# A streaming log-sum-exp prefix: straight-line engines, and a last store split between two queues

## The chip, the cores and the metric

The kernel runs on one core of a Trainium2 chip. The metric is device microseconds of one execution, as the device measures it. Each kernel was run several times, and medians are quoted. The profile is of one of these executions, and its span (first to last instruction) is some 1.7 us shorter than the time of the same execution.

## The reference

A running log-sum-exp along the second axis of a float32 tensor of 8 x 4096 x 2048. It is 268.44 MB in and as much out.

```python
out[:, 0, :] = x[:, 0, :].copy()
for t in range(1, S):
    mx = np.maximum(out[:, t - 1, :], x[:, t, :])
    out[:, t, :] = mx + np.log(np.exp(out[:, t - 1, :] - mx) + np.exp(x[:, t, :] - mx))
```

## The kernel before

The input is cut into 64 tiles of 512 rows: 128 partitions, 4 rows each, 2048 columns, 4 MB in and 4 MB out ("8 MB per tile" below counts both). Six buffers rotate. SyncE (SP) loads. ScalarE (ACT) takes the exponential, VectorE adds the four rows of a partition, TensorE adds what lies in the partitions above and carries the sum into the next tile. VectorE joins the two, ScalarE takes the logarithm and issues the store. SP, ACT and DVE run in loops, so that each wait subtracts its count from the semaphore:

```python
def take(engine, s, n):
    event(engine, [(s, n)], [(s, "sem-sub-imm", n)])
...
with nc.Block() as block:
    ...
    @block.sync
    def _(sp):
        ...
        sp.dma_start(out=ti[0][:, 0:2, :], in_=x_v[0][:, 0:2, :]).then_inc(top, 16)
        sp.dma_start(out=ti[0][:, 2:R, :], in_=x_v[0][:, 2:R, :]).then_inc(loaded[0], 16)
        ...
        with sp.Fori(1, turns + 1) as j:
            for n in range(NI):
                take(sp, stored[n], 16)
                load(x_v[bass.ds(j * NI + n, 1)][0], n)
```

The last two tiles leave as column halves. Such a half has 4 KB rows in HBM:

```python
def store(n, dst, turn, h=None):
    cols = slice(0, D) if h is None else half(h)
    act.wait_ge(logs, 2 * turn + (2 if h is None else h + 1))
    act.dma_start(
        out=dst[:, :, cols], in_=ti[n % NI][:, :, cols]
    ).then_inc(stored[n % NI], 16)
...
for h in range(2):
    ln(NT - 1, h, NT - 1 - first)
    store(NT - 1, o_v[NT - 1], NT - 1 - first, h)
```

The softmax here doesn't subtract the row's maximum and nothing guards it: scores larger than these inputs give would overflow.

## Time and profile before

| | before |
|---|---|
| median of the first 3 runs | 1250.83 us (1250.73 to 1252.3) |
| span of the profiled execution | 1249.03 us |
| end of the last data packet in it | 1247.33 us |
| from there to the end of the span ("exit") | 1.70 us |
| DMA rate from 10 to 1208 us | 433 GB/s, all 16 engines busy |

How to read it: the DMA engines are full from 2 us on (first packet at 2.04 us, share 1.00 from 2 to 10 us), so only three things can move the time. They are the start of the first load, the rate of the middle, and the last few microseconds, in which the DMA engines finish one after another. The prediction below shows the lines.

The trace does not number the DMA engines. What it has are packets with start, length, size and queue, and a four-byte completion packet per engine at the end of each transfer (1040 for 65 loads, 16 each). While the engines are full (share 1.00 from 10 to 1208 us), an engine's next packet starts as the one before it ends, so packets can be strung together.

### The profile page before, as it was taken

To read this page: it belongs to the slowest core of one execution; us is meant where nothing else is said; L and a number is where in the kernel's file an instruction comes from. 1 tells how busy PE (TensorE), PEld (TensorE's weight loads), DVE (VectorE), ACT (ScalarE), POOL (GpSimd) and SP (SyncE) were. 2 spreads that over 40 slices of the span, in tenths; PEclk is the share of its full clock that TensorE was granted. 3 is DMA by queue.
4 is the path that set the end of the run, shared out by engine and by line. 5 is a ranking of instruction groups with operands and counts; after the bars stand their busy time and mean duration, and the time that the engine had idled before them with its cause. 6 is when DMAs were issued, how large, how long until landed. Compare 5 with 4: busy or idle time off the path is not lost. (4 is left out here: it accounts for less than half of the span.)

```text
span 1249.0 us, 3456 instructions
## 1 busy us (share of the span) xinstructions
PE 650.8 (52%) x960; PEld 215.3 (17%) x960; DVE 1023.0 (82%) x512; ACT 907.2 (73%) x258; POOL 1.1 (0%) x8
## 2 busy tenths in 40 slices
PE   3556455554566545655455544565545564465541
PEld 1112111111112111211111111121111121111110
DVE  4999978778787787887878878778787787877873
ACT  5897866867768677686776866867768677686774
POOL 0000000000000000000000000000000000000000
PEclk9897778786887868778778786777878878678785
DMA  9999999999999999999999999999999999999998
GB/s 403 420 436 430 433 430 437 433 431 434 430 436 434 431 433 430 437 434 430 434 430 436 436 430 434 430 436 437 428 434 431 436 436 429 434 430 436 436 430 354
DMA packets 20409, 537.01 MB, mean 430 GB/s; under 512 B 2096, under 2 KB 2096, under 8 KB 4144
## 3 DMA queue, kind: packets, MB, share of 16 engines
q1 hardware_dynamic: 9360, 268.44, 49.9%
q10 hardware_dynamic: 11040, 268.44, 49.9%
q8 instruction: 7, 0.11, 0.0%
q14 instruction: 2, 0.02, 0.0%
HBM read 268.44 MB, written 268.44 MB: 430 GB/s over the span
## 5 line engine op out<-in xcount | busy, mean ns | idle before, releaser
L136 ACT ACTIVATE ti<-ti 128x4096 f32<-128x4096 f32 (+1 forms) x128 | 452.6, 3582 | 310.2 <-ACTq L59 304.2
L232 DVE TENSOR_TENSOR ti<-ti 128x1024 f32<-128x1024 f32 x384 | 464.7, 1224 | 200.0 <-ACT ti L136 191.3
L241 DVE TENSOR_TENSOR ti<-ti,ps 128x4096 f32<-128x4096 f32 x128 | 560.0, 4416 | 9.4 <-PE ps L208 9.0
L208 PE MATMUL ps<-ti,before 128*128 128x512 f32 x512 | 380.4, 895 | 342.6 <-DVE ti L232 342.1
L142 ACT ACTIVATE ti<-ti 128x4096 f32<-128x4096 f32 x128 | 455.4, 3602 | 11.5 <-PE ps L197 6.0
L197 PE MATMUL ps<-ti,last 128*128 128x512 f32 x448 | 270.6, 735 | 234.2 <-DVE ti L241 234.2
L208 PEld LDWEIGHTS ps<-ti,before 128*128 128x128 f32 x512 | 128.7, 279 | 609.0 <-DVE ti L232 500.9
L197 PEld LDWEIGHTS ps<-ti,last 128*128 128x128 f32 x448 | 86.6, 214 | 401.8 <-DVE ti L241 334.7
L159 ACT ACTIVATE ti<-ti 128x4096 f32<-128x4096 f32 x1 | 3.6, 3616 | 6.5 <-ACTq L59 6.5
L32 ACT ACT_TABLE_LOAD x1 | 1.3, 1283 | 0.8 <-PEq L274 0.8
L103 POOL TENSOR_SCALAR_AFFINE_SELECT last<-last 128x128 f32<-128x128 f32 x1 | 0.3, 296 | 0.0
L98 POOL TENSOR_SCALAR_AFFINE_SELECT before<-before 128x128 f32<-128x128 f32 x1 | 0.3, 295 | 0.1
L95 POOL MEMSET last<- 128x128 f32 x1 | 0.2, 206 | 0.0
L94 POOL MEMSET before<- 128x128 f32 x1 | 0.2, 205 | 0.5 <-SPq L77 0.5
L274 POOL MEMSET const-bfloat16-1.0<- 128x1 bf16 x1 | 0.1, 103 | 0.0
L274 POOL MEMSET const-uint8-127<- 128x1 uint8 x1 | 0.1, 103 | 0.0
L274 POOL MEMSET const-float32-0.0<- 128x1 f32 x1 | 0.1, 99 | 0.3 <-issue 0.3
L274 POOL MEMSET const-float32-1.0<- 128x1 f32 x1 | 0.1, 99 | 0.0
## 6 DMA issues: line engine op xcount, KB each, us to landing
ti<-in_x_dram SPq DMA_DIRECT2D x63, 4096.0 KB, 38.4
out_dram<-ti ACTq DMA_DIRECT2D x62, 4096.0 KB, 44.0
out_dram<-ti ACTq DMA_DIRECT2D x4, 2048.0 KB, 12.9
ti<-in_x_dram SPq DMA_DIRECT2D x2, 2048.0 KB, 9.7
```

The lines of the kernel that those rows point to most:

```text
L32: nc.scalar.preload_act_table_set("natural_log_exp_and_others")
L94: g.memset(before[:], 1.0).then_inc(ones, 1)
L98: g.affine_select(out=before[:], in_=before[:], compare_op=mybir.AluOpType.is_ge, fill=0.0, base=-1, pattern=[[1, P]], channel_multiplier= ...
L103: g.affine_select(out=last[:], in_=last[:], compare_op=mybir.AluOpType.is_ge, fill=0.0, base=-(P - 1), pattern=[[0, P]], channel_multiplier=1,
L136: act.activation(t[:, rows, half(h)], t[:, rows, half(h)], ACT.Exp).then_inc(exps[h], 1)
L142: act.activation(t[:, :, half(h)], t[:, :, half(h)], ACT.Ln)._wait_ge(carried[h], turn + 1).then_inc(logs, 1)
L159: act.activation(ti[0][:, 0:2, :], ti[0][:, 0:2, :], ACT.Exp)
L197: m = pe.matmul(ps[(n + 1) % 2][:, sl], last[:], ti[n % NI][:, R - 1, sl], start=True, stop=False, skip_group_check=True,)
L208: m = pe.matmul(ps[n % 2][:, sl], before[:], ti[n % NI][:, R - 1, sl], start=n % NBLK == 0, stop=True, skip_group_check=True,)
L232: a = dve.tensor_add(t[:, r, half(h)], t[:, r - 1, half(h)], t[:, r, half(h)])
L241: dve.tensor_add(t[:, :, half(h)], t[:, :, half(h)], ps[n % 2][:, half(h)].unsqueeze(1).to_broadcast([P, R, HALF]),)._wait_ge(ahead[h], n ...
L274: nc = _bacc.Bacc("TRN2", target_bir_lowering=False, num_devices=1)
```

## The change

Its intent has three parts. The loops of SP, ACT and DVE are unrolled and the subtracting waits become plain ones. Tile 62 leaves whole, and tile 63 by rows (row 0, row 1, rows 2 and 3). And the last of these, 2 MB, is split by partitions: 60 of them leave through GpSimd's queue, which is meant to use 15 of the 16 DMA engines and leave out the slow one. A copy of five partitions at the head is meant to place the gap.

```diff
+    def parts(n):
+        return [slice(0, 1), slice(1, 2), slice(2, R)] if n == NT - 1 else [slice(0, R)]
+    PASS = slice(64, 124)
...
+        for rows, c in ((slice(0, 2), top), (slice(2, R), loaded[0])):
+            c(nc.sync.dma_start(out=ti[0][:, rows, :], in_=x_v[0][:, rows, :]), 16)
         with nc.Block() as block:
...
+                aimed(g.dma_start(out=spare[0:5, 64:80], in_=spare[0:5, 0:16]), 16)
+                g.wait_ge(aimed.s, aimed.n)
+                g.wait_ge(final.s, 1)
+                rows = parts(NT - 1)[-1]
+                passed(g.dma_start(
+                    out=o_v[NT - 1][PASS, rows, :], in_=ti[(NT - 1) % NI][PASS, rows, :]
+                ), 16)
...
             def _(sp):
-                with sp.Fori(1, turns + 1) as j:
-                    for n in range(NI):
-                        take(sp, stored[n], 16)
-                        load(x_v[bass.ds(j * NI + n, 1)][0], n)
+                for n in range(1, NT):
+                    i = n % NI
+                    if n >= NI:
+                        sp.wait_ge(stored[i].s, n // NI * 16)
+                    loaded[i](sp.dma_start(out=ti[i][:], in_=x_v[n]), 16)
...
             def _(act):
+                                for own in (
+                                    [slice(0, PASS.start), slice(PASS.stop, P)] if end else [slice(0, P)]
+                                ):
+                                    stored[n % NI](act.dma_start(
+                                        out=o_v[n][own, rows, :], in_=t[own, rows, :]
+                                    ), 16)
...
+        for c in [*stored, passed]:
+            nc.sync.wait_ge(c.s, c.n)
```

(Cut to its core. The same is done to DVE's and ACT's loops and to all waits.)

More of the change, by code (lines that the diff above doesn't have):

```diff
@@ L36 @@
     R = 4
+    NI = 6
+    FD = 512
+    HALF = D // 2
     NBLK = S // (P * R)
     NT = B * NBLK
-    FD = 512
-    NI = 6
-    HALF = D // 2
-    assert NI % 2 == 0 and NBLK % 2 == 0 and D == 4 * FD
+    assert D == 4 * FD
     pool = ctx.enter_context(tc.tile_pool(name="io", bufs=1))
@@ L47 @@
     last = pool.tile([P, P], f32, name="last", tag="last")
+    spare = pool.tile([P, P], f32, name="spare", tag="spare")
     ti = [pool.tile([P, R, D], f32, name=f"ti{i}", tag=f"ti{i}") for i in range(NI)]
@@ L52 @@
     o_v = out.rearrange("b (k p r) d -> (b k) p r d", p=P, r=R)
-    def half(h):
-        return slice(h * HALF, (h + 1) * HALF)
-    def event(engine, waits, updates):
-        engine.add_instruction(mybir.InstEventSemaphore(
-            name=f"I-{nc.next_id()}", engine=engine.engine, ins=[], outs=[],
-            sync_info=mybir.SyncInfo(
-                on_wait=[mybir.SyncWait(
-                    sync_type="semaphore", id=s.num, ant_name=s.name,
-                    wait_mode="sem-ge-imm", wait_value=n,
-                ) for s, n in waits],
-                on_update=[mybir.SyncUpdate(
-                    sync_type="semaphore", id=s.num, ant_name=s.name,
-                    update_mode=mode, update_value=n,
-                ) for s, mode, n in updates],
-            ),
-        ))
@@ L73, in take, with __init__, __call__ @@
-    def take(engine, s, n):
-        event(engine, [(s, n)], [(s, "sem-sub-imm", n)])
+    half = [slice(h * HALF, (h + 1) * HALF) for h in range(2)]
+    def parts(n):
+        return [slice(0, 1), slice(1, 2), slice(2, R)] if n == NT - 1 else [slice(0, R)]
+    PASS = slice(64, 124)
+    class Count:
+        def __init__(self, name):
+            self.s, self.n = tc.alloc_semaphore(name), 0
+        def __call__(self, inst, by=1):
+            inst.then_inc(self.s, by)
+            self.n += by
+            return self.n
@@ L77, with counts @@
     with tc.tile_critical():
-        def sems(name, n):
-            return [nc.alloc_semaphore(f"{name}{i}") for i in range(n)]
-        ones, shaped, logs, top = (
-            sems(s, 1)[0] for s in ("ones", "shaped", "logs", "top")
-        )
-        loaded, stored = sems("loaded", NI), sems("stored", NI)
-        exps, chain, sums, ahead, joined, carried = (
-            sems(s, 2) for s in ("exps", "chain", "sums", "ahead", "joined", "carried")
-        )
+        def counts(name, n):
+            return [Count(f"{name}{i}") for i in range(n)]
@@ new lines @@
+        ones, shaped, logs, top, chain, aimed, final, passed = (
+            Count(s) for s in ("ones", "shaped", "logs", "top", "chain", "aimed", "final", "passed")
+        )
+        loaded, stored = counts("loaded", NI), counts("stored", NI)
+        exps, sums, ahead, joined, carried = (
+            counts(s, 2) for s in ("exps", "sums", "ahead", "joined", "carried")
+        )
+        for rows, c in ((slice(0, 2), top), (slice(2, R), loaded[0])):
+            c(nc.sync.dma_start(out=ti[0][:, rows, :], in_=x_v[0][:, rows, :]), 16)
@@ L93, in _ @@
             def _(g):
-                g.memset(before[:], 1.0).then_inc(ones, 1)
-                g.memset(last[:], 1.0).then_inc(ones, 1)
-                g.wait_ge(ones, 2)
-                g.affine_select(
+                ones(g.memset(before[:], 1.0))
+                ones(g.memset(last[:], 1.0))
+                ones(g.memset(spare[:], 0.0))
+                g.wait_ge(ones.s, ones.n)
+                shaped(g.affine_select(
                     out=before[:], in_=before[:], compare_op=mybir.AluOpType.is_ge, fill=0.0,
@@ L100, in _ @@
                     base=-1, pattern=[[1, P]], channel_multiplier=-1,
-                ).then_inc(shaped, 1)
-                g.affine_select(
+                ))
+                shaped(g.affine_select(
                     out=last[:], in_=last[:], compare_op=mybir.AluOpType.is_ge, fill=0.0,
                     base=-(P - 1), pattern=[[0, P]], channel_multiplier=1,
-                ).then_inc(shaped, 1)
+                ))
+                aimed(g.dma_start(out=spare[0:5, 64:80], in_=spare[0:5, 0:16]), 16)
@@ L108, in _ @@
+                g.wait_ge(aimed.s, aimed.n)
[4 more added lines that the diff above has]
+                ), 16)
             @block.sync
             def _(sp):
-                def load(src, n):
-                    sp.dma_start(out=ti[n][:], in_=src).then_inc(loaded[n], 16)
-                sp.dma_start(out=ti[0][:, 0:2, :], in_=x_v[0][:, 0:2, :]).then_inc(top, 16)
@@ L115, in _ @@
-                sp.dma_start(out=ti[0][:, 2:R, :], in_=x_v[0][:, 2:R, :]).then_inc(loaded[0], 16)
-                for n in range(1, NI):
-                    load(x_v[n], n)
-                turns = (NT - NI) // NI
-                with sp.Fori(1, turns + 1) as j:
-                    for n in range(NI):
-                        take(sp, stored[n], 16)
-                        load(x_v[bass.ds(j * NI + n, 1)][0], n)
-                for n in range((turns + 1) * NI, NT):
-                    take(sp, stored[n % NI], 16)
-                    load(x_v[n], n % NI)
@@ L126, in _, with exp @@
-                for n in range(NT - NI, NT):
-                    take(sp, stored[n % NI], 32 if n >= NT - 2 else 16)
+                for n in range(1, NT):
[3 more added lines that the diff above has]
+                    loaded[i](sp.dma_start(out=ti[i][:], in_=x_v[n]), 16)
             @block.scalar
             def _(act):
-                def exp(n, h, rows=slice(0, R)):
+                def exp(n):
                     t = ti[n % NI]
-                    if h == 0:
-                        take(act, loaded[n % NI], 16)
-                    act.activation(
-                        t[:, rows, half(h)], t[:, rows, half(h)], ACT.Exp
-                    ).then_inc(exps[h], 1)
@@ L140, in ln @@
-                def ln(n, h, turn):
-                    t = ti[n % NI]
-                    act.activation(
-                        t[:, :, half(h)], t[:, :, half(h)], ACT.Ln
-                    )._wait_ge(carried[h], turn + 1).then_inc(logs, 1)
-                def store(n, dst, turn, h=None):
-                    cols = slice(0, D) if h is None else half(h)
-                    act.wait_ge(logs, 2 * turn + (2 if h is None else h + 1))
-                    act.dma_start(
-                        out=dst[:, :, cols], in_=ti[n % NI][:, :, cols]
-                    ).then_inc(stored[n % NI], 16)
@@ L153, in settle @@
-                def settle(turns):
-                    take(act, carried[0], turns)
-                    take(act, carried[1], turns)
-                    take(act, logs, 2 * turns)
-                take(act, top, 16)
-                act.activation(ti[0][:, 0:2, :], ti[0][:, 0:2, :], ACT.Exp)
-                exp(0, 0, slice(2, R))
-                exp(0, 1, slice(2, R))
-                turns = (NT - 2) // NI
-                with act.Fori(0, turns) as j:
-                    for n in range(1, NI + 1):
-                        exp(n, 0)
-                        exp(n, 1)
-                        ln(n - 1, 0, n - 1)
-                        ln(n - 1, 1, n - 1)
-                        store(n - 1, o_v[bass.ds(j * NI + (n - 1), 1)][0], n - 1)
-                    settle(NI)
@@ L171, in _ @@
-                first = turns * NI
-                for n in range(first + 1, NT):
-                    up, turn = n - 1, n - 1 - first
-                    exp(n, 0)
-                    if n < NT - 1:
-                        exp(n, 1)
-                    ln(up, 0, turn)
-                    if n == NT - 1:
-                        store(up, o_v[up], turn, 0)
-                        exp(n, 1)
-                    ln(up, 1, turn)
-                    store(up, o_v[up], turn, 1 if n == NT - 1 else None)
@@ L183, in _ @@
-                for h in range(2):
-                    ln(NT - 1, h, NT - 1 - first)
-                    store(NT - 1, o_v[NT - 1], NT - 1 - first, h)
-                settle(NT - first)
+                    lo = 0
+                    if n == 0:
+                        lo = 2
+                        act.activation(t[:, :lo], t[:, :lo], ACT.Exp)._wait_ge(top.s, 16)
+                    for h in range(2):
+                        a = act.activation(t[:, lo:, half[h]], t[:, lo:, half[h]], ACT.Exp)
+                        if h == 0:
+                            a._wait_ge(loaded[n % NI].s, (n // NI + 1) * 16)
+                        exps[h](a)
@@ new lines, in ln @@
+                def ln(n):
+                    t = ti[n % NI]
+                    for h in range(2):
+                        for rows in parts(n) if h else [slice(0, R)]:
+                            end = n == NT - 1 and rows.stop == R and h == 1
+                            c = final if end else logs
+                            c(act.activation(
+                                t[:, rows, half[h]], t[:, rows, half[h]], ACT.Ln
+                            )._wait_ge(carried[h].s, n + 1))
+                            if h:
+                                act.wait_ge(c.s, c.n)
+                                for own in (
[4 more added lines that the diff above has]
+                                    ), 16)
@@ L188, in _ @@
+                exp(0)
+                for n in range(NT):
+                    if n + 1 < NT:
+                        exp(n + 1)
+                    ln(n)
             @block.tensor
@@ L192, in carry @@
                     if n % NBLK == NBLK - 1:
-                        event(pe, [(joined[h], n + 1)], [(carried[h], "sem-add-imm", 1)])
+                        pe.wait_ge(joined[h].s, n + 1)
+                        pe.sem_inc(carried[h].s, 1)
                         return
@@ L201, in carry @@
                         if c == 2 * h:
-                            m._wait_ge(joined[h], n + 1)
-                    m.then_inc(carried[h], 1)
+                            m._wait_ge(joined[h].s, n + 1)
+                    carried[h](m)
                 def triangle(n, h):
@@ L212, in triangle @@
                         if c == 2 * h:
-                            m._wait_ge(sums[h], n + 1)
-                    m.then_inc(ahead[h], 1)
-                pe.wait_ge(shaped, 2)
+                            m._wait_ge(sums[h].s, n + 1)
+                    ahead[h](m)
+                pe.wait_ge(shaped.s, shaped.n)
                 for n in range(NT):
@@ L222, in _ @@
                         carry(n, h)
-                for h in range(2):
-                    take(pe, sums[h], NT)
-                    take(pe, joined[h], NT)
             @block.vector
@@ L229, in local @@
                 def local(n, h):
-                    t = ti[n]
+                    t, cols = ti[n % NI], half[h]
                     for r in range(1, R):
-                        a = dve.tensor_add(t[:, r, half(h)], t[:, r - 1, half(h)], t[:, r, half(h)])
+                        a = dve.tensor_add(t[:, r, cols], t[:, r - 1, cols], t[:, r, cols])
                         if r == 1:
-                            a._wait_ge(exps[h], n + 1)
+                            a._wait_ge(exps[h].s, n + 1)
                         else:
-                            a._wait_ge(chain[h], (R - 2) * n + r - 1)
-                        a.then_inc(*((chain[h], 1) if r < R - 1 else (sums[h], 1)))
+                            a._wait_ge(chain.s, chain.n)
+                        (chain if r < R - 1 else sums[h])(a)
                 def join(n, h):
-                    t = ti[n]
-                    dve.tensor_add(
-                        t[:, :, half(h)], t[:, :, half(h)],
-                        ps[n % 2][:, half(h)].unsqueeze(1).to_broadcast([P, R, HALF]),
-                    )._wait_ge(ahead[h], n + 1).then_inc(joined[h], 1)
-                def turn(tiles):
-                    for n in range(tiles):
-                        for h in range(2):
-                            local(n, h)
-                        for h in range(2):
-                            join(n, h)
-                    for h in range(2):
-                        take(dve, exps[h], tiles)
-                        take(dve, chain[h], (R - 2) * tiles)
-                        take(dve, ahead[h], tiles)
-                with dve.Fori(0, NT // NI):
-                    turn(NI)
-                turn(NT % NI)
+                    t, cols = ti[n % NI], half[h]
+                    joined[h](dve.tensor_add(
+                        t[:, :, cols], t[:, :, cols],
+                        ps[n % 2][:, cols].unsqueeze(1).to_broadcast([P, R, HALF]),
+                    )._wait_ge(ahead[h].s, n + 1))
+                for n in range(NT):
+                    for h in range(2):
+                        local(n, h)
+                    for h in range(2):
+                        join(n, h)
+        for c in [*stored, passed]:
+            nc.sync.wait_ge(c.s, c.n)
 _INS = ['x']
```

## The prediction

> **What bounds the kernel now.** I read the page first: engine shares, then the row of DMA slices, then the queues.
>
> ```profile
> PE 650.8 (52%) x960; PEld 215.3 (17%) x960; DVE 1023.0 (82%) x512; ACT 907.2 (73%) x258; POOL 1.1 (0%) x8
> ...
> DMA  9999999999999999999999999999999999999998
> ...
> DMA packets 20409, 537.01 MB, mean 430 GB/s; under 512 B 2096, under 2 KB 2096, under 8 KB 4144
> ...
> q1 hardware_dynamic: 9360, 268.44, 49.9%
> q10 hardware_dynamic: 11040, 268.44, 49.9%
> q8 instruction: 7, 0.11, 0.0%
> ```
>
> No compute engine is full; the 16 DMA engines are, in every slice but the last. Loads (q1) and stores (q10) each take half of them. The work is 268.44 MB in and 268.44 MB out, so the time is a head before the first byte, 537 MB through full DMA engines, and a tail. Next the stretches, to see whether the stream ever thins:
>
> ```profile
> 0.00:10.00 10.00, 0.00 (x0) 0.00 (x0) 0.00 (x0) 2.66 (x2) 1.09 (x8) 1.00 0.80 315
> 10.00:1208.00 1198.00, 641.52 (x948) 212.27 (x948) 1005.82 (x504) 883.03 (x251) 0.00 (x0) 0.79 1.00 433
> 1208.00:1244.00 36.00, 9.25 (x12) 3.03 (x12) 17.13 (x9) 21.48 (x6) 0.00 (x0) 0.65 0.99 418
> 1244.00:1249.00 5.00, 0.00 (x0) 0.00 (x0) 0.00 (x0) 0.00 (x0) 0.00 (x0) 0.50 0.11 47
> ```
>
> The last two columns are DMA share and GB/s. From 10 to 1244 us the DMA is full (1.00 and 0.99). In the last 5 us it is at 0.11 while no engine computes. Magnified, the last 10 us in slices of 0.25 us:
>
> ```profile
> DMA  9999999989999999987655330000000000000000
> GB/s 426 393 442 410 426 410 442 442 360 442 393 459 410 393 442 410 442 360 311 246 213 229 131 131 16 33 16 33 33 16 33 16 33 0 0 0 0 0 0 0
> ```
>
> The rate steps down from 1243.5 to 1245 as engines finish one after another, then stays at 16 to 33 GB/s until 1247.25. A sixteenth of 430 GB/s is 27: **one DMA engine works alone for 2.2 us.** The trace's packets say the same. Each transfer ends with a four-byte completion packet per DMA engine; for the last store these come at 1243.35 us for the first, 1245.13 for the fifteenth and 1247.32 for the sixteenth. In the first load the sixteenth was only 0.17 us behind the fifteenth; over the last 35 tiles that distance grows by some 0.06 us per tile of 8 MB, except where another engine is delayed. So I read one engine as 0.3% slower than the rest (0.06 of 19.36 us per tile), always the last, and its share of the bytes sets the end. Last, the timeline:
>
> ```profile
> 1231.86 0.54 ACTq L149 DMA_DIRECT2D out_dram<-ti  x1
> 1232.54 3.62 ACT L142 ACTIVATE ti<-ti 128x4096 f32<-128x4096 f32 x1 [0.71 <-PEq L59]
> 1236.18 0.54 ACTq L149 DMA_DIRECT2D out_dram<-ti  x1
> ```
>
> The last logarithm ends at 1236.16, eleven microseconds before the last byte. The arithmetic at the end is hidden by a queue of stores.
>
> [...] The trace only has 16-way transfers (1040 completion packets for 65 loads, 1056 for 66 stores)[...]; nor does it say which engine is slow. [...]
>
> **The change part by part.**
>
> *Straight-line engines.* Loops and subtracting waits go from SP, ACT and DVE. Their instructions are not on the path: DVE has 18% idle, ACT 27%, DMA none. Worth 0 in itself. [...] one 16 KiB packet costs one DMA engine 0.6 us of its time (two 16 KiB rows of the load took 611 ns at the median each). Hit on a late engine it shows, on an early one not: an estimate of +0.2 us.
>
> *First loads before the block.* SP's first issue stands at 1.03 us, after a no-op at 0.80 and a branch at 0.87. Without the branch it can go at some 0.82: −0.2 us for the whole stream.
>
> *Tile 62 whole, tile 63 by rows.* Before, the last two tiles leave as four column halves of 512 packets of 4 KB. Such a half took the slow engine 4.94 us (completions at intervals of 4.96, 4.95, 4.91, 4.93), where half of a whole-row 4 MB store took 4.87 (9.74 for tile 61). Larger packets: 4 x 0.07 = −0.3 us. Also the second exponential of tile 63 is no longer behind a logarithm of tile 62, so the last joins and logarithms come some 4 us earlier, the pieces' issues in between included; hidden anyway. Store 62 is now issued once, near 1223; store 61's first engine has finished about 1223.3 and an issue takes 1.0 us to its first byte (1.03 to 2.04 at the head). A gap of 0.7 us on the earliest engines falls into their slack.
>
> *Sixty partitions through GpSimd.* The last store is 2 MB, 128 KB per engine. Now ACT sends partitions 0 to 63 on 16 engines, 64 KB each; 124 to 127 as 16 KB on four engines; GpSimd 60 x 16 KB, 64 KB on 15 engines. If the left-out one is the slow one it carries 64 KB less: 64 KB at its own rate (4.87 us per 128 KB) = 2.4 us, which brings it from 1247.32 to 1244.9. The fifteenth, at 1245.13, then sets the end; with the extra 16 KB (0.6 us) if it is one of the four: 1245.1 to 1245.7. Gain 2.2 or 1.6, say −1.9 us. The GpSimd transfer starts near 1235, well inside the queue.
>
> *Exit.* After the last wait, SP passes a block barrier from 1247.75 to 1247.96; it now comes before the waits: −0.2 us. GpSimd's queue may need some of it back in its own drain.
>
> Sum: +0.2 − 0.2 − 0.3 − 1.9 − 0.2 = −2.4 us, thus 1248.4 if all works.
>
> **The rivals.**
> *Wrong engine left out.* If [...]the slow engine is another one here, the slow engine still carries its 128 KB. For: nothing in the trace names it. Against: the copy at the head exists only to place it. Then −0.5 us: 1250.3.
> [...]
> *Slow descriptors.* GpSimd's generation late or its drain long at the exit: there are some 10 us of queue before it shows[...].
> *Compute starves the DMA* because the store of 62 waits for both halves: above, 0.7 us against 1.8 us of slack between first and fifteenth engine. Small.
>
> **Range and chances.** All works 1248.4; [...]wrong engine 1250.3. Weighted about 0.5, 0.25 and 0.25 this is 1249.2; I take 1249.1, and 1247.6 to 1250.7 as the range. Two per cent is 25 us: neither a gain nor a loss of that size has a place in a stream where everything touched lies in the first 2 and the last 15 us. Faster 0.005, same 0.99, slower 0.005.
>
> **What would show it.** Right: in the last 10 us no long stretch at 16 to 33 GB/s; the last completions within some 0.6 us of one another; a GpSimd queue of about 0.98 MB; first issue at 0.8 us; the middle still at 433 GB/s. Wrong engine: the lone tail of 2 us remains. [...] The prediction is wrong if the middle changes rate (instruction fetches that delay an engine more than 0.6 us each), or if GpSimd's queue holds up the end.

The text is as recorded, but for the marked cuts: passages on how the hardware works that no trace or run of this case shows. That 60 partitions of GpSimd use 15 engines, four partitions each, was measured later (e9), and so was that the four remaining ones use four (in the trace of after, ACT's stores have 1060 completion packets, 66 x 16 + 4). One rival is called "the slow piece" below. It had a piece of 64 partitions run slower than a transfer of all 128, with 1.2 us of the gain lost: 1249.6, at a chance of 0.25, which is in the 1249.2. Its sign was to be that the last slices stand near half rate over all engines. The trace of before has no such piece to show it.

## The result, and the profile after

| | before | after |
|---|---|---|
| median, same rounds | 1251.26 us (1250.73 to 1252.3) | 1252.94 us (1252.71 to 1253.41) |
| span of the profiled execution | 1249.03 us | 1251.69 us |
| last data packet | 1247.33 us | 1249.30 us |
| exit | 1.70 us | 2.39 us |

The ratio is 1.0014, with a 95% interval of 0.9999 to 1.0028: the same at 2%. A ratio here is the mean time of one kernel's runs over that of the other's of the same rounds, so not quite the ratio of the medians. Executions over 1.5% slower than the fastest of the same kernel are left out of the means. For the kernel before, that mean is lifted in some jobs by single runs of up to 1256.7 us. Its median in the five later jobs was 1250.76 to 1250.97 us. I therefore compare medians, and mostly within one job. The change lost 1.7 to 2.2 us, where a gain was predicted and the range ended at 1250.7.

The page of the kernel after, with the rows that answer to those shown of before:

```profile
PE 646.0 (52%) x960; PEld 213.1 (17%) x960; DVE 1023.4 (82%) x512; ACT 907.9 (73%) x260; POOL 2.3 (0%) x11
...
DMA  9999999999999999999999999999999999999998
...
DMA packets 18935, 537.06 MB, mean 429 GB/s; under 512 B 2152, under 2 KB 2152, under 8 KB 2152
...
q1 hardware_dynamic: 9360, 268.44, 49.8%
q10 hardware_dynamic: 9448, 267.46, 49.6%
q0 software_dynamic: 112, 0.98, 0.2%
q8 instruction: 7, 0.11, 0.0%
q14 instruction: 8, 0.07, 0.0%
```

The work is the same. The packets of 4 KB are gone (2152 under 8 KB, 4144 before). Queue q0 is GpSimd's 0.98 MB. The last row is new in size: eight instruction packets of 8 KB, against two before.

The stretches of the kernel after (the last two columns are DMA share and GB/s):

```profile
10.00:1208.00 1198.00, 637.21 (x948) 210.31 (x948) 1005.77 (x504) 883.17 (x251) 0.00 (x0) 0.79 1.00 433
1208.00:1244.00 36.00, 8.74 (x12) 2.74 (x12) 17.63 (x9) 21.77 (x8) 0.54 (x1) 0.63 1.00 408
1244.00:1249.00 5.00, 0.00 (x0) 0.00 (x0) 0.00 (x0) 0.00 (x0) 0.00 (x0) 0.50 0.38 136
```

The middle is untouched, 433 GB/s. In the second stretch the share is 1.00 (0.99 before), but the rate is 408 where it was 418: **the engines are busy and move less.** What was not moved there is moved after 1244 us. The kernel after from 1239 to 1249 us, in slices of 0.25 us:

```profile
DMA  6999491999699693988966619846334314101010
GB/s 262 459 459 426 164 623 66 328 426 393 262 164 524 229 361 131 426 197 229 360 164 229 229 66 360 229 131 262 131 131 197 131 66 197 66 0 66 0 66 0
```

The rate sags from 1242 us on, over many engines, and there is no clean step. From the trace's packets: a row of 16 KB takes one DMA engine 611 ns at the median (256 such packets in the first two loads). In this tail 32 of 128 such packets took over 733 ns (1.2 times), the longest 2820 ns. In the kernel after, the last seven completion packets come at 1247.29, 1247.45, 1247.89, 1248.06, 1248.36, 1248.68 and 1249.30.

The timeline of the end of ACT and GpSimd (POOL), and the last data wait of SP:

```profile
1232.20 1.91 ACT L145 ACTIVATE ti<-ti 128x2048 f32<-128x2048 f32 x1 [0.41 <-ACT ti L145]
1234.14 2.04 ACTq L153 DMA_DIRECT2D out_dram<-ti  x2
1234.72 0.54 POOL L113 DMA_DIRECT2D out_dram<-ti  x1 [1232.02 <-ACT ti L145]
...
SPq L225 <- DMA out_dram<-ti: 0.9, 1, 0.9
```

The last logarithm ends at 1234.11, 2 us earlier than before; the prediction had some 4, and neither matters behind the queue of stores. GpSimd's store is issued at 1234.72. Its first packet in the trace is at 1238.73, 4.0 us after the issue (3.9 us for the copy at the head, from 2.07 to 5.95), still four microseconds before the first engines run dry.

### The profile page after: what moved, and what is told of

It is laid out like the page before. It is cut to its first block, busy times and chain, and to the rows that moved or that the text cites. A ratio compares the mean times of both kernels' runs of the same rounds, so it can differ in the third digit from the quotient of the medians.

```text
span 1251.7 us, 2923 instructions
## 1 busy us (share of the span) xinstructions
PE 646.0 (52%) x960; PEld 213.1 (17%) x960; DVE 1023.4 (82%) x512; ACT 907.9 (73%) x260; POOL 2.3 (0%) x11
## 2 busy tenths in 40 slices
DMA packets 18935, 537.06 MB, mean 429 GB/s; under 512 B 2152, under 2 KB 2152, under 8 KB 2152
## 4 chain that ended last, share of the span: by engine, by line
DMA 79%; ACT 13%; DVE 4%; PE 1%; DVEq 0%; issue 0%; ACTq 0%; POOLq 0%; SPq 0%; PEldq 0%
DMA ti<-in_x_dram 41%; DMA out_dram<-ti 39%; ACT ti L145 7%; ACT ti L134 7%; DVE ti L213 2%; DVE ti L204 2%; PE ps L184 1%; DVEq L89 0%; PE ps L173 0%; ACTq L153 0%; POOLq L89 0%; SPq L87 0%; PEldq L169 0%; SPq L251 0%; POOLq L111 0%
## 5 line engine op out<-in xcount | busy, mean ns | idle before, releaser
L134 ACT ACTIVATE ti<-ti 128x4096 f32<-128x4096 f32 (+1 forms) x128 | 452.5, 3582 | 308.4 <-DMA ti<-in_x_dram 306.7
L145 ACT ACTIVATE ti<-ti 128x4096 f32<-128x4096 f32 (+1 forms) x130 | 456.0, 3550 | 10.8 <-PE ps L173 7.5
L132 ACT ACTIVATE ti<-ti 128x4096 f32<-128x4096 f32 x1 | 3.6, 3616 | 6.3 <-DMA ti<-in_x_dram 6.3
```

Of the source, the lines that this page charges most:

```text
L132: act.activation(t[:, :lo], t[:, :lo], ACT.Exp)._wait_ge(top.s, 16)
L134: a = act.activation(t[:, lo:, half[h]], t[:, lo:, half[h]], ACT.Exp)
L145: c(act.activation(t[:, rows, half[h]], t[:, rows, half[h]], ACT.Ln)._wait_ge(carried[h].s, n + 1))
```

## The experiments

The theory formed after the result: a transfer from part of the partitions is slow in itself, whichever queue sends it (called A). Rivals were: GpSimd's queue itself is slow or late (C); the copy does not place the left-out engine (D), so that nothing is gained; the four remaining partitions (A2); and what the unrolled code does to the DMA engines and to the exit. The letters A, A2, C and D are those of the expectations; other letters there are what their own text says. "After" is 1252.94 us throughout.

All kernels were correct within the comparison. Medians in us, beside the median of before in the same job; the last two columns are of the profiled execution:

| run | what it is | median | before | last data | exit |
|---|---|---|---|---|---|
| e1 | after, no GpSimd, last rows whole | 1250.90 | 1250.80 | 1246.66 | 2.52 |
| e2 | e1 with the small copy | 1251.02 | 1250.80 | 1246.35 | 2.39 |
| e3 | pieces moved: GpSimd's from the middle, ACT's beside it | 1252.44 | 1250.80 | 1247.93 | 2.39 |
| e4 | same pieces, all by ACT | 1253.87 | 1250.80 | 1249.77 | 2.39 |
| e5 | GpSimd with 64 partitions | 1252.66 | 1250.97 | 1247.39 | 2.41 |
| e6 | staircase of big transfers | 1292.04 | 1250.97 | 1287.94 | 2.38 |
| e7 | before, with rows at the end | 1250.57 | 1250.97 | 1247.42 | 1.82 |
| e8 | row 3 by GpSimd, all partitions | 1250.86 | 1250.86 | 1246.49 | 2.53 |
| e9 | probe with tiny copies | 1251.58 | 1250.86 | 1247.86 | 2.00 |
| e10 | every second partition by GpSimd | 1253.58 | 1250.86 | 1249.54 | 2.38 |
| e11 | two halves of 64 by ACT | 1253.19 | 1250.76 | 1248.99 | 2.40 |
| e12 | after without the copy | 1253.38 | 1250.76 | 1250.30 | 2.39 |
| e13 | HBM halves (wrong) | 1250.74 | 1250.80 | 1246.60 | 2.51 |
| e14 | SBUF halves (wrong) | 1253.28 | 1250.80 | 1249.08 | 2.40 |

### e1: without GpSimd's part

```diff
-                aimed(g.dma_start(out=spare[0:5, 64:80], in_=spare[0:5, 0:16]), 16)
-                g.wait_ge(aimed.s, aimed.n)
-                ... (GpSimd's store)
-                                    [slice(0, PASS.start), slice(PASS.stop, P)] if end else [slice(0, P)]
+                                    [slice(0, P)]
```

> The changed kernel without any DMA from GpSimd: no small copy, and the last rows of tile 63 leave as one 128-partition transfer from ACT. Theory A (the 64- and 60-partition pieces are slow[...], and GpSimd's DMA lengthens the exit): the span falls by 2.5 to 3.5 us against the changed kernel, to 0.3 to 1 us under the kernel before; last data near 1246.5 us, exit near 1.3 us, no packet longer than its usual time in the tail. Rival B (the straight line or the row-wise pieces, with store 62 issued whole, cost the time): it stays within 0.7 us of the changed kernel.

Measured: 1250.90 us (1250.77 to 1252.74), ratio to before 1.0004 [0.9991, 1.0018]. The 2 us are gone with the split: 1252.94 − 1250.90 = 2.04 us, or 1.6 us if each is first set against before in its own job (+1.68 and +0.10). No 16 KB packet of the tail took over 733 ns. The exit stayed at 2.5 us, so the longer exit isn't GpSimd's: that part of the expectation fell, and the gain over after was smaller than the 2.5 to 3.5 us that it named. Two windows of e1, to be set beside those of after (the second pair):

```profile
1239.00:1244.00 5.00, 0.00 (x0) 0.00 (x0) 0.00 (x0) 0.00 (x0) 0.00 (x0) 0.50 1.01 431
1244.00:1249.00 5.00, 0.00 (x0) 0.00 (x0) 0.00 (x0) 0.00 (x0) 0.00 (x0) 0.50 0.09 38
```

```profile
1239.00:1244.00 5.00, 0.00 (x0) 0.00 (x0) 0.00 (x0) 0.00 (x0) 0.00 (x0) 0.50 1.04 324
```

Both are full (1.01 and 1.04), but after moves 324 GB/s where e1 moves 431. In five microseconds that is (431 − 324) x 5 us = 0.54 MB, more than a quarter of the last store, which then comes later.

e1 also shows what the unrolled code does to the engines. A block of 8 KB comes in at 102, 219, 406, 704, 717, 1028 and 1209 us. Below, "the drifting engine" is the slow one of the prediction, whose lag grows from tile to tile. The engine that comes second to last at the end has, in its load completions (loads counted from 0), this lag behind the fastest:

```
lag of one engine in e1, us:  0.31 (load 6) -> 0.97 (load 8) -> 1.83 (load 23) -> 2.67 (load 39) -> 3.49 (load 55)
8 KB packets at, us:                        102             406              717              1028
```

Each of these four packets is recorded with 309 ns, yet sets the same engine back by 0.66 (the first) to 0.86 us. This makes a second late engine of it. The packets at 219 and 704 us fell on another engine, which lost 0.55 us each time. The last completions are:

```
before  1245.10 1245.11 1245.14 1247.33
e1      1244.73 1244.78 1246.34 1246.66
e7      1245.04 1245.08 1245.10 1247.42
```

### e2: with the copy, without GpSimd's store

```diff
-                g.wait_ge(final.s, 1)
-                rows = parts(NT - 1)[-1]
-                passed(g.dma_start(
-                    out=o_v[NT - 1][PASS, rows, :], in_=ti[(NT - 1) % NI][PASS, rows, :]
-                ), 16)
-                                    [slice(0, PASS.start), slice(PASS.stop, P)] if end else [slice(0, P)]
+                                    [slice(0, P)]
```

> As the run without GpSimd DMAs, but with the small copy at the head kept. Theory A: what GpSimd's queue costs at the exit alone; the interval from the last store's completion to the end of the span is 2.0 us as in the changed kernel, against 1.3 to 1.4 without, so this run is 0.5 to 0.8 us slower than the run without GpSimd. Rival: the longer exit came from the late transfer still draining (GpSimd's drain took 13.8 us); then this run equals the one without to 0.2 us.

Measured: 1251.02 us (1250.45 to 1251.15), ratio 1.0002 [0.9988, 1.0015]. The copy costs nothing that shows, and the exit is 2.39 us with it as it is 2.52 without. An effect of GpSimd's queue on the exit isn't there; the expectation on that was a miss.

### e3 and e5: pieces moved, GpSimd's from the middle and ACT's from both ends

```diff
-    PASS = slice(64, 124)
+    PASS = slice(32, 92)                      # e5: slice(32, 96)
-                                    [slice(0, PASS.start), slice(PASS.stop, P)] if end else [slice(0, P)]
+                                    [slice(0, 32), slice(96, P), slice(92, 96)] if end else [slice(0, P)]
                                               # e5: [slice(0, 32), slice(96, P)]
```

> The changed kernel with GpSimd's sixty partitions moved from 64-123 to 32-91, and ACT's pieces 0-31, 96-127 and 92-95. Bytes per queue, engine counts and the copy are as in the changed kernel[...]. Theory A[...]: 16 KB packets of the tail return to 611 ns from up to 2 us, the last data comes 1.5 to 3 us earlier, the span falls by as much. Rival C (a late or slow GpSimd queue, or the wrong DMA engine left out, sets the end): the span stays within 0.7 us of the changed kernel.

> The changed kernel, but GpSimd takes 64 partitions (32 to 95) on 16 DMA engines and ACT the other 64 in two pieces of 32, so every engine has 128 KB of the last store, as in one 128-partition transfer, and there is no 4-partition remainder. Moving the partitions alone left 1.4 us over the run with the copy only. Theory A2 (those 1.4 us are the 16 KB that the remainder adds to four engines, a late one among them, 0.6 us, and the rest contention between the two queues): this run is 0.6 to 1.0 us faster than the run with the partitions moved. Rival C2 (GpSimd's queue itself is slow): it stays within 0.3 us of it.

Measured: e3 1252.44 us (1251.65 to 1253.25), ratio 1.0014 [1.0001, 1.0028]; e5 1252.66 us (1251.26 to 1253.11), ratio 1.0002 [0.9981, 1.0022]. e3 is only 0.5 us under after, where much more was expected: a miss. In e3's trace 12 of 128 packets took over 733 ns, where after has 32. e5 has no remainder of four partitions and is no faster, so the remainder isn't supported as the cause. Its six runs are far apart, so it isn't ruled out as a small part. Taken alone, both results are what the rivals C and C2 forecast, GpSimd's queue being slow; e4 and e8 below decide against them.

### e4: the same pieces, all from ACT

```diff
-                                    [slice(0, PASS.start), slice(PASS.stop, P)] if end else [slice(0, P)]
+                                    [slice(0, PASS.start), slice(PASS.stop, P), PASS] if end else [slice(0, P)]
                                     (and nothing by GpSimd)
```

> The changed kernel's same three pieces (partitions 0-63, 124-127, 64-123), all issued by ACT, with no GpSimd DMA. [...] Theory A[...]: [...]the last data comes 3 to 5 us later than with one 128-partition transfer, packets of 16 KB take near 1.2 us. Rival C (GpSimd is what is slow): it equals the run without GpSimd to 0.7 us.

Measured: 1253.87 us (1253.21 to 1254.44), ratio 1.0024 [1.001, 1.0038], in the same job as e1: +3.0 us over it. GpSimd has no part in it and the loss is all there and more. Of 128 packets of 16 KB, 74 took over 733 ns, with a median of 975. The pieces cost, not the queue.

### e6: a staircase of big transfers

```diff
+    STAIR = [slice(s, s + w) for s, w in zip([0, 15, 29, 42, ...], [*range(15, 0, -1), 8])]
...                                 # the store of tile 58 by these, a GpSimd store of 60 partitions in tile 59
+                                    else STAIR if n == 58 else [slice(0, P)]
```

> A probe for the numbers of the DMA engines, not a candidate. The store of tile 58 leaves as sixteen transfers of 15, 14, ... 1 and 8 partitions from ACT[...]. Tile 59 leaves with partitions 64 to 123 from GpSimd, 4 packets on each of 15 engines. Theory D (the copy aims past the slow engine): the engine whose packets take 1218 ns on average, and the one that carries the instruction fetches, each still have 4 packets of GpSimd's queue, and the engine without any is a third. Rival (aimed well): the slow one has none. The time may be several us longer; it says nothing.

Measured: 1292.04 us in one run, of unknown state. One of the runs of the kernel before in this job took 1291.77 us (slow) at an unchanged clock, so the total alone would prove little. But the trace says where e6 lost its 41 us. Here are its windows around the staircase, which ACT issues from 1146 us on, and then one of e1:

```profile
10.00:1150.00 1140.00, 602.34 (x900) 199.01 (x900) 956.84 (x480) 840.63 (x239) 0.00 (x0) 0.79 1.00 433
1160.00:1200.00 40.00, 21.64 (x32) 6.91 (x30) 27.68 (x13) 20.56 (x7) 0.54 (x1) 0.80 1.00 365
```

```profile
1160.00:1200.00 40.00, 25.46 (x35) 8.03 (x33) 33.18 (x18) 29.46 (x9) 0.00 (x0) 0.76 1.00 433
```

Up to 1150 us e6 is as fast as the others. Once the pieces run, its engines are just as busy (1.00) but move only 365 GB/s; the tail of after shows the same. This points to the pieces, in one run. For its own question, the numbers of the engines, e6 is inconclusive, as the crowded packets couldn't be told apart by engine; e9 does it with less. One thing could be counted: the transfers of 15, 14, ... 1 and 8 partitions have 15 + 14 + ... + 1 + 8 = 128 completion packets, as many as they have partitions.

### e7: the kernel before, with tile 62 whole and tile 63 by rows

```diff
-                    if n < NT - 1:
-                        exp(n, 1)
+                    exp(n, 1)
...
-                    store(up, o_v[up], turn, 1 if n == NT - 1 else None)
+                    store(up, o_v[up], turn)
+                for i, rows in enumerate((slice(0, 1), slice(1, 2), slice(2, R))):
+                    ln(n, 1, turn, rows)
+                    act.wait_ge(logs, 2 * turn + 2 + i)
+                    act.dma_start(
+                        out=o_v[n][:, rows, :], in_=ti[n % NI][:, rows, :]
+                    ).then_inc(stored[n % NI], 16)
```

> The kernel before, loops and all, with only the last two tiles changed: tile 62 stored whole, tile 63 by rows (one, one, two), as in the run without GpSimd. Theory E (the straight line costs 0.7 us at the exit, and its instruction fetches make a second DMA engine late, but that one does not set the end): exit 1.7 us as before, last data 0.4 to 0.7 us before that of the kernel before, span 0.3 to 0.8 us under both. Rival (the longer exit comes from something else than the straight line): exit 2.4 us, and the time of the run without GpSimd.

Measured: 1250.57 us (1250.46 to 1250.98), ratio 0.9986 [0.9966, 1.0006]. Its median is 0.40 us under before's of the same job, and it is the fastest of all kernels here, but not by a margin that the interval settles. The exit is 1.82 us, there are two small instruction packets as before, and there is one late engine, not two. The last data of its profiled execution (the slowest of its six) is at 1247.42 us, no earlier than before's 1247.33. So the longer exit and the second late engine both come with the unrolled kernel. (It also moved the first loads and the last waits out of the block, and e7 doesn't separate that for the exit.)

### e8: the same amount through GpSimd, but from all partitions

```diff
-                    out=o_v[NT - 1][PASS, rows, :], in_=ti[(NT - 1) % NI][PASS, rows, :]
+                    out=o_v[NT - 1][:, 3:4, :], in_=ti[(NT - 1) % NI][:, 3:4, :]
...                                 # ACT sends row 2 of all partitions
```

> The changed kernel, with the last 2 MB split by rows, not by partitions: ACT sends row 2, GpSimd row 3, each over all 128 partitions, 1 MB, 16 DMA engines. [...]every engine has 128 KB, as with one transfer by ACT; only the queue differs. Theory A (the partition pieces are what is slow): the tail is that of the run with the copy only, within 0.4 us in time, no 8 KB packet much over 309 ns. Rival C (GpSimd's queue itself costs the time, by its late start or its descriptors): it stays 1 to 2 us above the run with the copy only.

Measured: 1250.86 us (1250.67 to 1251.59), ratio 0.9999 [0.9985, 1.0012]. The windows of e8 and its GpSimd queue:

```profile
q0 software_dynamic: 176, 1.05, 0.2%
...
1239.00:1244.00 5.00, 0.00 (x0) 0.00 (x0) 0.00 (x0) 0.00 (x0) 0.00 (x0) 0.50 1.01 424
```

1.05 MB go through GpSimd and the window moves 424 GB/s, near e1's 431 and not after's 324. The rival that GpSimd's queue comes late or slowly is refuted as the cause of the loss. The queue is not the matter; which partitions a transfer takes is.

### e9: a probe for the numbers of the engines

```diff
+                g.wait_ge(logs.s, 2 * 51)
+                for i in range(4):
+                    passed(g.dma_start(out=spare[64:124, 100 + 16 * i:116 + 16 * i], in_=spare[64:124, 0:16]), 16)
+                    g.wait_ge(passed.s, passed.n)
...
+                    if n == 55:
+                        sp.wait_ge(ones.s, 3)
+                        for w in range(15, 0, -1):
+                            stair(sp.dma_start(out=spare[0:w, 180 + 16 * w:196 + 16 * w], in_=spare[0:w, 0:16]), 16)
```

SP sends tiny copies of 15, 14, ... 1 partitions, 64 bytes each. GpSimd sends four tiny copies of 60 partitions. The packets were strung together into 16 engines by their joints in time. An engine is named here by how many of SP's tiny packets it got: with 15 it is number 0, with 14 number 1, with none number 15.

> A probe for the numbers of the DMA engines[...]: the run with the copy only, and near tile 55 fifteen tiny transfers (64 bytes a partition) of 15, 14, ... 1 partitions from SP[...], and near tile 51 four copies of 60 partitions from GpSimd, one after the other. Theory D (the copy aims past the late engines): the first of the four leaves out an engine that is neither of the two that finish last. [...] Rival: the first leaves out one of the two late engines. Time within 0.5 us of the run with the copy only.

Measured: 1251.58 us in one run, 0.56 over e2 where at most 0.5 was forecast. That the sets of engines are nested is measured, by the counts; the numbers are only names for these counts. So numbered:

```
drifting engine (32 KB packets 1216 to 1218 ns on average) 11 of the tiny packets -> number 4
engine that the 8 KB instruction packets set back          12                     -> number 3
engine left out by GpSimd, four times of four               0                     -> number 15
```

**The slow engine is number 4. The one that GpSimd leaves out is number 15.** In all four copies it had a completion packet of its own (16 bytes) and no data; engines 0 to 14 had four partitions each. The gap did not move from copy to copy. By these counts the slow engine keeps its full 128 KB of the last store (four packets of 16 KB from each queue), and the one that is relieved had time. The numbers are those of this run's chip, but the trace of after agrees: its drifting engine, followed by the joints from 1170.91 us (32 KB packets of 1217.6 ns, 1213 on most others up to 1223 us), carries 16 KB packets of GpSimd's queue at 1240.40 and 1242.21 us. It was not left out there either.

### e12: after without the copy

```diff
-                aimed(g.dma_start(out=spare[0:5, 64:80], in_=spare[0:5, 0:16]), 16)
-                g.wait_ge(aimed.s, aimed.n)
```

> The changed kernel without the small copy at the head; the sixty partitions still leave by GpSimd. Theory D2 (GpSimd spreads 60 partitions four to an engine over engines 0 to 14 and always leaves out 15, as all four tiny copies of the probe did, so the copy places nothing): the time is that of the changed kernel, 1252.9 us, to 0.5 us. Rival[...]: another engine is left out, and the time moves by 0.6 us or more either way.

Measured: 1253.38 us (1253.05 to 1254.40), ratio 1.0021 [1.0008, 1.0035]. It is within 0.5 us of after, as forecast, though each set against before in its own job they are 0.9 apart (+2.62 and +1.68). So the time alone doesn't settle whether the copy places anything. In e9, with the same copy at the head, GpSimd's four copies did not leave out the slow engine; and the copy brings no gain.

### e11: two halves of the partitions, by ACT alone

```diff
-                                    [slice(0, PASS.start), slice(PASS.stop, P)] if end else [slice(0, P)]
+                                    [slice(0, 64), slice(64, P)] if end else [slice(0, P)]
                                     (and nothing by GpSimd)
```

> ACT alone, no GpSimd DMA: the last 2 MB as two transfers of 64 partitions (0 to 63, 64 to 127), so every engine has the same 128 KB as with one transfer, and there is no remainder. Theory A (a transfer of 64 neighbouring partitions crowds 16 engines[...]): 2 to 3 us slower than the run without GpSimd (1250.9 us), with many 16 KB packets near 1.2 us, nearly all of what the run with three pieces by ACT lost (3.0 us). Rival F (the 4-partition remainder and the number of issues were what cost it): within 0.6 us of 1250.9.

Measured: 1253.19 us (1253.09 to 1254.07), ratio 1.0021 [1.0007, 1.0035]: 2.3 us over e1. All 16 engines take part in each half (1072 completion packets for 67 stores), no remainder, no GpSimd, one issue more. The two windows of e11:

```profile
1239.00:1244.00 5.00, 0.00 (x0) 0.00 (x0) 0.00 (x0) 0.00 (x0) 0.00 (x0) 0.50 1.05 275
1244.00:1249.00 5.00, 0.00 (x0) 0.00 (x0) 0.00 (x0) 0.00 (x0) 0.00 (x0) 0.50 0.71 180
```

The engines are busy (1.05) at 275 GB/s, and still at 0.71 after 1244. The median packet of 16 KB took 1247 ns, twice 611.

### e13 and e14: which side is crowded

A half of the partitions is also a half of the tile's rows in HBM, so e11 leaves open which side is crowded. Both kernels below write rows to wrong places, inside the last tile. The comparison with the reference passed all the same, presumably since rows so late in a running log-sum-exp differ little.

```diff
+# e13: all 128 partitions, each transfer into one half of the tile's rows in HBM
+    tile63 = out.rearrange("b (k g p q) d -> (b k) g q p d", g=2, p=P, q=2)[NT - 1]
+                                        stored[n % NI](act.dma_start(
+                                            out=tile63[r // 2, r % 2], in_=t[:, r, :]
+                                        ), 16)
+# e14: 64 partitions at a time, each spread over the whole tile in HBM
+                                for j in range(2 if end else 1):
+                                        out=o_v[n][:, 2 + j, :].rearrange("(p q) d -> p q d", q=2) if end else ...,
+                                        in_=t[64 * j:64 * j + 64, rows, :] if end else t[:, rows, :],
```

> Wrong result on purpose (rows of tile 63 permuted). ACT alone, tile 63 as four transfers of one row of all 128 partitions, the first two into the first half of the tile's rows in HBM, the last two into the second half. Each transfer [...]writes only one half of the range, as the 64-partition pieces do. Theory A (the SBUF side is crowded): within 0.5 us of the run without GpSimd (1250.9 us), 8 KB packets at 309 ns. Rival H (the HBM side is crowded): 2 us slower or more.

> Wrong result on purpose (rows of tile 63 permuted). ACT alone, the last 2 MB from partitions 0 to 63 and then 64 to 127, as in the run with two halves, but each half is written over the whole range of the tile in HBM, in 8 KB rows like an ordinary one-row store. Theory A (SBUF side): as slow as the two halves, 1253.2 us, to 0.6 us, with many 8 KB packets near twice 309 ns. Rival H (HBM side): within 0.5 us of 1250.9.

Measured: e13 1250.74 us (1250.37 to 1251.47), ratio 1.0000 [0.9986, 1.0014]; e14 1253.28 us (1253.15 to 1254.66), ratio 1.0022 [1.001, 1.0035], on the same chip. From 1239 to 1249 us, e13 and then e14, in slices of 0.25 us:

```profile
DMA  9898999989999799988975010111000000000010
GB/s 492 360 393 360 492 492 393 393 360 492 492 393 393 328 492 492 459 360 360 426 295 229 33 66 33 66 66 66 33 33 0 0 0 0 0 0 0 0 33 0
```

```profile
DMA  9979695997939969899695999977979969783400
GB/s 393 361 262 426 229 426 131 262 262 197 328 98 295 262 164 295 197 197 229 197 361 197 328 328 295 295 164 164 262 164 262 197 131 229 164 229 131 164 33 33
```

e13 holds some 400 GB/s up to 1244 us, and from 1244.5 has only its late engines. e14 has the same digits of busy share with some 230 GB/s for many microseconds. From 1239 us on, a packet of 8 KB took a median of 309 ns in e13 and of 626 in e14. **The crowding is on the SBUF side,** shown by the pair: HBM halves cost nothing, SBUF halves 2.5 us.

### e10: every second partition

If a block of neighbours is what crowds, then every second partition should not.

```diff
-    PASS = slice(64, 124)
+    PASS = slice(1, 120, 2)
-                                    [slice(0, PASS.start), slice(PASS.stop, P)] if end else [slice(0, P)]
+                                    [slice(0, P, 2), slice(121, P, 2)] if end else [slice(0, P)]
```

> The changed kernel, with GpSimd's sixty partitions taken as every second one (1, 3, ... 119), ACT's 64 as 0, 2, ... 126, and 121 to 127 by twos as the remainder. Bytes, engine counts and order are those of the changed kernel[...]. Theory A: hardly any 16 KB packet over 1.2 times its usual 611 ns, and 1.0 to 1.8 us faster than the changed kernel; what stays over the run with the copy only is the remainder's 0.6 us on a late engine. Rival C: within 0.6 us of the changed kernel.

Measured: 1253.58 us (1251.59 to 1253.69), ratio 1.0015 [1.0001, 1.0028]: a miss, no better than after. 42 of 128 packets took over 733 ns. Why it is no better was not shown. What of the loss in e3 and e10 is the pieces and what the remainder was not separated.

## Why the prediction was wrong

The mechanism that it called the bound was right, and so was the middle. That the ratio would stay within 2% was right too; little else was possible, as all that was touched lies in the first 2 and the last 15 us. The gain that it put on the last store was not there, and the term came with the opposite sign.

1. **First loads before the block: forecast −0.2, measured 0.** SP's first issue is at 1.033 us before and at 1.029 after. The branch that was to fall away stands there still, since it is not the block's.
2. **Straight-line engines: forecast +0.2, under-sized.** That longer code brings more instruction packets was right (8 small ones for 2), but the step counted what a packet takes (0.6 us for 16 KB, so 0.3 for 8 KB), and it is 0.55 to 0.86 us that an engine loses by 8 KB, four times on the same one. The trace of before could have told: its 8 KB block at 1150.8 us sets an engine back by 0.85 us, and its 16 KB block at 1087.9 us by 1.28. For the same reason the slow engine is not "always the last" there: up to load 29, engines that took such blocks are later. It stays under the drifting engine's lag, so e1 hardly shows it in the time. But it makes the second late engine of e1 (1246.34 beside 1246.66). On the unrolled kernel, relieving only the drifting engine can bring no more than the 0.3 us between the two. The 2.2 us that the prediction read off the kernel before were no longer to be had.
3. **Larger packets and rows: forecast −0.3, sign not settled.** e7's median is 0.40 us lower, which its interval doesn't settle. The prediction's intervals are misread a little: from one last completion to the next the trace of before has 4.98 to 5.00 us for the halves and 9.73 for tile 61, so the same working gives −0.5. e1's last data is 0.67 us earlier than before's, in one profile each and with the unrolled code; e7's profile doesn't show it.
4. **Sixty partitions through GpSimd: forecast −1.9, measured +2.0. This is the step that failed.** "If the left-out one is the slow one it carries 64 KB less: 64 KB at its own rate (4.87 us per 128 KB) = 2.4 us, which brings it from 1247.32 to 1244.9. The fifteenth, at 1245.13, then sets the end". The runs put two things in its place. The left-out engine is number 15 and the slow one number 4, in four copies of four (e9); that GpSimd's store would leave out the slow one was not shown by any trace. And the split by partitions makes the SBUF side crowded, which costs 2.3 us with ACT alone (e11), 2.5 us in e14, and 1.6 to 2.0 us between e1 and after.
5. **Exit: forecast −0.2, measured +0.7.** The barrier does come before the waits. But from the last data to the end it is 2.38 to 2.53 us in all unrolled kernels but the probe, with and without GpSimd, and 1.70 and 1.82 in the two with loops. The cause is only argued: these kernels fetch an 8 KB block of instructions within the exit (in e1 at 1248.8 us, in after at 1251.3), the ones with loops do not, and e9, whose fetch came at 1212 us, exits in 2.00. Against it as the whole cause: in e1 SyncE already stands idle for 0.41 us (1247.74 to 1248.15), before the recorded fetch begins.

The terms close by construction, in the profiled executions, and show the sizes: −0.67 (last data, e1 against before) + 2.64 (last data, after against e1) + 0.69 (exit, 2.39 against 1.70) = +2.66, and the spans differ by 1251.69 − 1249.03 = 2.66.

Of the **rivals**, "wrong engine" and "the slow piece" were both right in what was measured, and both at once. The prediction weighed them as alternatives, each taking part of the gain. It gave the slow piece 1.2 us, by the hope that the two pieces overlap; the pieces cost 1.6 to 2.5. With "wrong engine" alone at its forecast 1250.3, the pieces' cost on top (1251.9 to 1252.8) is past the top of the range at 1250.7; the exit is lost besides. "Slow descriptors" fell with e8, and "compute starves the DMA" was harmless, as forecast.

The sign of "the slow piece" was there: from 1242 to 1246 us the engines are at 0.84 and move 258 GB/s, for 433 in the middle. The lone tail of "wrong engine" is hidden under it. GpSimd's queue did not hold up the end: its drain took 13.8 us, but was over at 1248.53, before the last data at 1249.30.

**What stays open.** Whether relieving engine 4 would gain anything: no transfer of these queues was found that leaves out engine 4 alone. Why pieces of part of the partitions are slow, and why every second partition is no better. What the exit's 0.7 us are. How the 2 us between e1 and after divide between ACT's and GpSimd's pieces and the four remaining partitions. And e7's 0.4 us are under what its interval settles.

## What to carry to other kernels

Here, with the DMA engines as the bound, a split of the last 2 MB by partitions to steer it between engines or queues cost 1.6 to 2.5 us (after, e11, e14). Cut by rows, with all 128 partitions in each piece, it cost nothing that shows (e8, 1250.86 us; e1, 1250.90). So try rows first. Before aiming at one engine, measure which one is late and which one a transfer leaves out; tiny copies with falling partition counts did that in one run (e9). And price a second late engine before counting on relief of the first (in e1, 1246.34 beside 1246.66 us).
